# Second FFN of a two-layer decoder: six groups of four hidden blocks by seven products, with the weight sums made ahead and kept in HBM

## The chip, the cores and the metric

The kernel runs on one core of a Trainium2 chip. Its time is the device time of one execution in microseconds; several runs give a median. A profile of one execution says what each engine did: TensorE (PE; its weight loads are PEld), VectorE (DVE), ScalarE (ACT), GpSimd (POOL) and SyncE (SP), which issues most of the transfers.

## The reference

A trunk of two layers over 256 tokens of width 2048, all in float32. Layer 0 mixes tokens by latent attention, layer 1 by dilated sliding-window attention with three head groups; each is followed by a feed-forward network with a short convolution. The part that matters here is that network:

```python
def conv_ffn(h, w_up, conv_w, conv_b, w_down):      # FFN_HIDDEN = 5632, CONV_WIDTH = 3
    u = h @ w_up                                     # 2048 -> 2 x 5632
    up = jnp.pad(u, ((0, 0), (CONV_WIDTH - 1, 0), (0, 0)))
    c = conv_b + up[:, 0:S] * conv_w[0]
    for j in range(1, CONV_WIDTH):
        c = c + up[:, j:j + S] * conv_w[j]
    gate, val = c[..., :FFN_HIDDEN], c[..., FFN_HIDDEN:]
    return (jax.nn.silu(gate) * val) @ w_down

# each layer: x += mixer(rmsnorm(x)); x += conv_ffn(rmsnorm(x)); final rmsnorm
```

## The kernel before

**Precision by splitting.** A float32 weight is used as two halves: `wh`, its value rounded to the fast matmul type (ScalarE copies it, L91), and `wl`, what is left (VectorE subtracts, L92). A product takes three matmuls: high by high, high by low, low by high. The activations are split in the same way and stay in SBUF.

**The weight ring.** `load` (L71 on) takes a tile `w` of 128x2048 (1 MB) from the pool `wst`, which has three, fills it by a transfer on SP's queue (L78), and splits it in two pieces of 1024 columns into `wh` and `wl`, of which the pool `wsp` has five each. A slot of `wst` is free again when VectorE has made the last `wl` from it. `load_tok2` (L146) does so for the value projections of the dilated stage, which come as quarters.

**A direct unit.** `proj` (L137) multiplies one loaded tile, 128 outputs by all 16 chunks of the input, for all 256 tokens: 16 matmuls of 512 columns with `wh` and 16 of 256 columns with `wl`, into one bank `pp` of PSUM. `unit` runs it, takes one entry of the list `steps` (other work to be put between, such as attention), and then empties the bank of the unit before (L213, L215 and what follows).

**The dilated stage** (layer 1's attention) goes over eight pairs of heads j. Each has 12 q and k units (three groups, q and k, two heads). Where j is even, four quarters of a value projection for two pairs follow each group's four units (L165 to L167). The attention of pair j runs from `steps` during pair j+1. Then comes the output projection.

**The FFN** has 44 hidden blocks of 128, each a gate and a value. `up(fb)` does a block by two direct units, the convolution and the gating; `down` adds a segment of some 11 finished blocks to the residual, 16 units, one for each block of outputs. Three groups of four blocks, the *fours* (`SEVEN = (12, 23, 34)`), go another way: the product of a 2x2 block matrix (two halves of the tokens by two halves of the input) with the four blocks' gate and value columns is made by seven block products instead of eight. The sums of activation blocks (`forms`) are made once at the start of the FFN. The sums of weight blocks are made by VectorE as the weights pass (`first`, `second`, L881 to L895), six products running side by side in six PSUM banks, one chunk pair after a `down` unit; the seventh follows (`third`). The products are 512-column matmuls with tokens in the rows (L853 to L855). `sums` and `last_sum` combine them, and `turn` (L947) transposes the result back, four 128x128 blocks for each hidden block, into the bank `pt` or `po`, from which the convolution reads (L958, L962).

**Order.** The framework's scheduler puts each engine's instructions in order before the run and adds the waits; TensorE's order follows the program. Transfers are issued by SP in program order, each waiting for its slot.

Of the kernel before, what the change touches and what calls it, by code (L numbers as in the profile page):

```python
# [40 lines left out]
SEGS = ((0, 10), (10, 21), (21, 32), (32, 44))  # L41
HALF = 4 * P
SEVEN = (12, 23, 34)
NEG = -1.0e30


# [6 lines left out]
def trunk_kernel(tc, x_d, pos_d, gain_d, conv_d, const_d, mask_d, wqa_d, wkva_d, wqb_d, wkvb_d, wo_d,  # L53
                 win_d, dwo_d, wup_d, wdn_d, out_d):
    nc = tc.nc
    with ExitStack() as ctx:
# [5 lines left out]
        tab = ctx.enter_context(tc.tile_pool(name="tab", bufs=1))  # L62
        work = ctx.enter_context(tc.tile_pool(name="work", bufs=4))
        small = ctx.enter_context(tc.tile_pool(name="small", bufs=4))
        pp = ctx.enter_context(tc.tile_pool(name="pp", bufs=4, space=PSUM))
        pss = ctx.enter_context(tc.tile_pool(name="pss", bufs=2, space=PSUM))
        pst = ctx.enter_context(tc.tile_pool(name="pst", bufs=1, space=PSUM))
# [55 lines left out]
        def proj(w, xs, n, since=0, upto=None, ps=None, onto=False):  # L123

            if ps is None:
                ps = pp.tile([P, 512], F32, name="pp", tag="pp")
            ks = range(since, upto or n)
            order = runs()  # L130
            if since == 0:
                state["own", id(ps)] = None if onto else order[0]
            own = state["own", id(ps)]
            for i in order:
                for k in ks:
                    w_k = w[k * P // WS][i][:, k * P % WS:k * P % WS + P]
                    nc.tensor.matmul(ps[:, i * T:], w_k, xs[k][:, :(2 - i) * T], start=(k == 0 and i == own),  # L137
                                     stop=(k == n - 1), skip_group_check=(i != own))
            return ps
# [48 lines left out]

        pending = []
        steps = []  # L190

        def nothing():
            pass
# [9 lines left out]
        def unit(project, evacuate):  # L203
            ps = project()
            if steps:
                steps.pop(0)()
            flush()
            pending.append((evacuate, ps))
# [146 lines left out]
        def split_act(ps):  # L355
            o = act.tile([P, 2 * T], F32R, name="a", tag="a")
            split_to(o, ps)
            return o
# [306 lines left out]
        def dilated():  # L665
# [20 lines left out]
            def project(j):  # L686
                h = {}

                def keep_qk(what, ps):
                    if what[1] == 0:  # L690
                        t = work.tile([P, T], F32, name="qk0", tag="tmp")
                    else:
                        t = att.tile([P, T], F32, name="qk", tag="qk", bufs=8)
                    rope(t, joined(ps), tabs["c"], tabs["s"], 32)
                    if what[1] == 0:
                        h[what] = att.tile([P, 2 * T], F32R, name="qks", tag="qks", bufs=4)
                        split_to(h[what], t)
                    else:
                        h[what] = t

                if j % 2 == 0:
                    state["v"] = {}
                values = h["v"] = state["v"]

                def keep_v(g, pss_):
                    for tt, ps in enumerate(pss_):
                        col = tabs["r"][:, tt:tt + 1]
                        if g == 0:
                            v = att.tile([P, 4 * T], F32R, name="vs", tag="vs", bufs=2)
                            split((v[:, :2 * T], v[:, 2 * T:]), ps, col)  # L710
                        else:
                            v = att.tile([P, 2 * T], F32, name="v", tag="v", bufs=4)
                            nc.scalar.activation(v, ps, AF.Copy, scale=col)
                        values[g, tt] = v

                for g in range(NG):
                    base = (j * NG + g) * 6
                    for i, what in enumerate("qk"):
                        for e in range(2):
                            w = load(win_d[base + 2 * i + e], D, tok=D)  # L720
                            unit(lambda: proj(w, xs, KC), lambda ps, what=what, g=g, e=e: keep_qk((what, g, e), ps))
                    if j % 2 == 0:
                        srcs = [(win_d[b + 4], win_d[b + 5]) for b in (base, base + 6 * NG)]
                        pss_ = [pp.tile([P, 512], F32, name="pp", tag="pp") for _ in range(2)]
                        for q in range(4):
                            w = load_tok2(srcs, q)

                            def quarter():
                                proj_tok2(w, pss_, xs, q)
                                return pss_  # L730

                            unit(quarter, (lambda p, g=g: keep_v(g, p)) if q == 3 else (lambda p: None))
                return h
# [56 lines left out]
                steps.extend([s0, nothing, together(s1, ta0, tb0), nothing, together(v0, ta1, tb1), v1])  # L790
            out_proj(dwo_d, os, G_FFN + KC, onto=True)


        def ffn(layer, goff, ready):
            gl = {}
# [228 lines left out]
            flush()  # L1024


        with tc.tile_pool(name="lat0", bufs=1) as lat, tc.tile_pool(name="att0", bufs=2) as att:
            mla()
        with tc.tile_pool(name="ffn0", bufs=1) as fpool:
# [11 lines left out]
            nc.scalar.activation(xt[c], xt[c], AF.Copy, scale=gains[:, G_FIN + c:G_FIN + c + 1])  # L1041

        with tc.tile_pool(name="ffn1", bufs=1) as fpool:
            ffn(1, G_FFN + KC, final)

        zero = work.tile([P, T], F32, name="zero", tag="lo", bufs=2)
        nc.vector.memset(zero, 0.0)
# [93 lines left out]
```

## Time and profile before

| | |
|---|---|
| three runs | 2674.61, 2674.69, 2675.85 us |
| profiled execution, span from first to last instruction | 2673.9 us |
| TensorE busy | 2657.8 us |
| VectorE busy | 2105.5 us |
| ScalarE busy | 1639.7 us |
| GpSimd busy | 24.7 us |
| mean transfer rate | 189 GB/s |
| read from HBM, written to it | 501.5 MB, 2.1 MB |

A busy share is the part of the span in which at least one instruction of that engine was running. Matmuls are pipelined, so the sum of their durations is longer than their busy time, and the step from one matmul's start to the next tells more than a duration. A row of a window gives its length, then the busy time and count of each engine, the granted clock, the share of the DMA engines' time and the rate. A row of the chain gives start, length and what ran. A row of a wait gives who waited for whom, the sum, the number of times and the longest.

### The profile page before, as it was taken

What the parts mean: (1) busy time and instruction counts of PE and PEld (TensorE: products, weight loads), DVE (VectorE), ACT (ScalarE), POOL (GpSimd) and SP (SyncE); (2) the same over time, 40 slices, a digit from 0 to 9 for tenths busy, and PEclk for the clock granted to TensorE, in tenths of its full rate; (3) what the DMA queues carried; (4) which work ended last, traced back from release to release, by engine and by line L of the source; (5) the groups of instructions that cost most, each with busy time, mean ns of one, the idle gap of its engine ahead of it and who ended that gap; (6) DMA issues with size and microseconds to landing.
All of it is one profiled execution on the core that took longest, in us unless ns stands there. A gap on an engine that the chain in (4) does not pass through costs nothing.

```text
span 2673.9 us, 40017 instructions
## 1 busy us (share of the span) xinstructions
PE 2657.8 (99%) x15167; PEld 2338.4 (87%) x15167; DVE 2105.5 (79%) x3630; ACT 1639.7 (61%) x2624; POOL 24.7 (1%) x39
## 2 busy tenths in 40 slices
PE   9999999999999999999999999999999999999998
PEld 7998888888888888898888888888888888888887
DVE  7987888898898876676577667667688889889885
ACT  6775666676666764444454444445666667666665
POOL 2000000000000000000000000000000000000000
PEclk9999999999999999999999999999999999999999
DMA  6335555656566565544544544544555575755744
GB/s 246 138 133 203 189 182 193 239 179 224 197 202 227 182 206 198 179 171 170 191 170 164 197 161 174 188 174 160 189 189 175 191 249 171 223 205 189 237 169 147
DMA packets 153553, 506.19 MB, mean 189 GB/s; under 512 B 11024, under 2 KB 86160, under 8 KB 118928
## 3 DMA queue, kind: packets, MB, share of 16 engines
q1 hardware_dynamic: 153072, 503.46, 54.9%
q8 instruction: 119, 1.95, 0.3%
q14 instruction: 74, 0.61, 0.1%
q10 hardware_dynamic: 288, 0.18, 0.0%
HBM read 501.50 MB, written 2.10 MB: 188 GB/s over the span
## 4 chain that ended last, share of the span: by engine, by line
PE 95%; DMA 1%; DVE 1%; issue 0%; ACT 0%; SPq 0%; DVEq 0%; ACTq 0%
PE pp L137 70%; PE pp L165 3%; PE pp L167 3%; PE pp L166 3%; PE ps L855 1%; PE ps L853 1%; PE ps L854 1%; DMA w<-in_wup 1%; PE pp L104 1%; PE pp L106 1%; PE pp L105 1%; PE pp L853 1%; PE pp L854 1%; PE pp L855 1%; PE po L781 1%; PE ps L744 1%
## 5 line engine op out<-in xcount | busy, mean ns | idle before, releaser
L92 DVE TENSOR_TENSOR wl<-w,wh 128x1024 fp32r<-128x1024 f32 (+3 forms) x802 | 881.9, 1110 | 371.0 <-ACT wh L91 228.1
L91 ACT ACTIVATE wh<-w 128x1024 fp32r<-128x1024 f32 (+3 forms) x802 | 770.9, 966 | 370.8 <-PE pp L137 220.7
L137 PE MATMUL pp<-xs,wh 128*128 128x512 f32 x3648 | 855.5, 390 | 0.0
L137 PEld LDWEIGHTS pp<-xs,wh 128*128 128x128 f32 x3648 | 677.1, 188 | 135.8 <-DVE xs L266 0.2
L137 PE MATMUL pp<-xs,wl 128*128 128x256 f32 x3648 | 465.3, 284 | 0.0
L137 PEld LDWEIGHTS pp<-xs,wl 128*128 128x128 f32 x3648 | 455.7, 191 | 9.3
L137 PE MATMUL pp<-a,wh 128*128 128x512 f32 x1920 | 459.7, 390 | 0.0
L137 PEld LDWEIGHTS pp<-a,wh 128*128 128x128 f32 x1920 | 357.7, 188 | 72.6
L137 PEld LDWEIGHTS pp<-a,wl 128*128 128x128 f32 x1920 | 248.1, 191 | 10.2
L137 PE MATMUL pp<-a,wl 128*128 128x256 f32 x1920 | 252.8, 283 | 0.0
L155 DVE TENSOR_TENSOR wl<-w,wh 128x1024 fp32r<-128x1024 f32 x96 | 116.2, 1218 | 62.3 <-ACT wh L154 50.3
L154 ACT ACTIVATE wh<-w 128x1024 fp32r<-128x1024 f32 x96 | 101.6, 1059 | 96.5 <-PE pp L166 50.0
L213 ACT ACTIVATE lo<-pp 128x256 f32<-128x256 f32 x225 | 85.7, 381 | 119.5 <-PE pp L137 119.4
L165 PE MATMUL pp<-wh,xs 128*128 128x512 f32 x384 | 150.0, 391 | 0.0
L167 PE MATMUL pp<-wl,xs 128*128 128x512 f32 x384 | 149.5, 389 | 0.0
L166 PE MATMUL pp<-wh,xs 128*128 128x512 f32 x384 | 149.4, 389 | 0.0
L962 DVE SCALAR_TENSOR_TENSOR cv<-upad,convs,cv 128x256 f32<-128x256 f32 x256 | 121.1, 481 | 18.3 <-ACT cv L958 15.9
L958 ACT ACTIVATE cv<-upad,convs 128x256 f32<-128x256 f32 x128 | 76.4, 598 | 72.7 <-DVE upad L972 71.0
L215 DVE TENSOR_TENSOR sum<-pp,lo 128x256 f32<-128x256 f32 x225 | 94.1, 418 | 0.2
L120 ACT ACTIVATE pp<-x 128x512 f32<-128x512 f32 x144 | 85.1, 591 | 13.6 <-DVE sum L215 6.8
L880 ACT ACTIVATE wh<-w 128x1024 fp32r<-128x1024 f32 x48 | 51.0, 1062 | 60.0 <-PE pp L137 43.0
L167 PEld LDWEIGHTS pp<-wl,xs 128*128 128x128 f32 x384 | 72.1, 188 | 15.0
(299 smaller groups left out, 3154.7 us busy)
## 6 DMA issues: line engine op xcount, KB each, us to landing
w<-in_wup SPq DMA_DIRECT2D x128, 1024.0 KB, 4.8
w<-in_win SPq DMA_DIRECT2D x96, 1024.0 KB, 4.8
w<-in_wup SPq DMA_DIRECT2D x96, 512.0 KB, 5.1
w<-in_win SPq DMA_DIRECT2D x96, 512.0 KB, 4.1
w<-in_wdn SPq DMA_DIRECT2D x64, 704.0 KB, 4.1
w<-in_wdn SPq DMA_DIRECT2D x32, 768.0 KB, 4.2
w<-in_wdn SPq DMA_DIRECT2D x32, 640.0 KB, 5.3
w<-in_wo SPq DMA_DIRECT2D x16, 1024.0 KB, 4.7
```

What stands on the lines that cost most here:

```text
L91: nc.scalar.activation(h, w[:, c:e], AF.Copy)
L92: nc.vector.tensor_sub(l, w[:, c:e], h.bitcast(F32))
L120: nc.scalar.activation(dst, chunk.unsqueeze(1).to_broadcast([P, 2, 2, P]), AF.Copy, scale=0.5)
L137: nc.tensor.matmul(ps[:, i * T:], w_k, xs[k][:, :(2 - i) * T], start=(k == 0 and i == own), stop=(k == n - 1), skip_group_check=(i != own))
L154: nc.scalar.activation(wh4, src, AF.Copy)
L155: nc.vector.tensor_sub(wl4, src, wh4.bitcast(F32))
L165: nc.tensor.matmul(ps, xh, wh, start=k == 0, stop=False)
L166: nc.tensor.matmul(ps, xl, wh, start=False, stop=False)
L167: nc.tensor.matmul(ps, xh, wl, start=False, stop=k == KC - 1)
L213: nc.scalar.activation(t, ps[:, T:], AF.Copy)
L215: nc.vector.tensor_add(u, ps[:, :T], t)
L962: nc.vector.scalar_tensor_tensor(o, v, convs[:, cw + j:cw + j + 1], o, op0=ALU.mult, op1=ALU.add)
```

## The change

Layer 0's FFN stays. Layer 1's becomes `ffn_ahead`: six fours go by seven products, two in each of three periods, and 20 blocks directly (12 at the start, 8 as `singles`).

The four sums of weight blocks no longer arise in the FFN. While layer 1's q and k weights are loaded, after every second load, `sums_ahead` takes one more tile of the ring, loads for one hidden block four chunks (512 columns) of each of its four weight parts (gate and value, first and second half of the input) into it by two transfers, adds in place four times on VectorE, and stores the tile to HBM by a transfer from POOL's queue: 48 times, 8 for each four. In the FFN each product then has its weights ready in HBM, raw for products 1, 2 and 3 and summed for 4 to 7. It is done in two halves of 12 matmuls, each with one 1 MB load and one split, the products one after the other in the two `ps` banks. The halves stand after units of `up` and `down`, up to two behind one unit, by lists written out by hand (`deal`, `put`). The 2x2 blocks divide the input in chunks 0 to 7 and 8 to 15 instead of even and odd ones, and the sums have other signs. The transposes stand behind two successive `down` units (7 and 8) for the first four of a period, behind `up` units for the second. At the end three early units of the last `down` replace two.

```diff
+FIRST = 12
+PERIODS = ((0, 11, 12, 16, (20, 21, 22)), (11, 22, 23, 27, (31, 32, 33)), (22, 33, 34, 38, (42, 43)))
...
+        def plan_sums(layer, fours):
+            for fb0 in fours:
+                t = made[layer, fb0] = hbm.tile([8, P, D], F32, name=f"sums_{layer}_{fb0}")
+                ahead.extend((t, layer, fb0, n) for n in range(8))
+
+        def sums_ahead():
+            if not ahead:
+                return
+            t, layer, fb0, n = ahead.pop(0)
+            f, q = n // 2, n % 2
+            w = wst.tile([P, D], F32, name="w", tag="w")
+            for h in range(2):
+                src = wup_d[layer, 2 * (fb0 + f) + h].rearrange("p (j c) -> p j c", j=2)[:, :, q * HALF:(q + 1) * HALF]
+                nc.sync.dma_start(w[:, h * WS:(h + 1) * WS].rearrange("p (j c) -> p j c", j=2), src)
+            b11, b21, b12, b22 = (w[:, ts(i, HALF)] for i in range(4))
+            nc.vector.tensor_add(b11, b11, b12)
+            nc.vector.tensor_add(b12, b12, b22)
+            nc.vector.tensor_add(b22, b11, b22)
+            nc.vector.tensor_add(b21, b22, b21)
+            nc.gpsimd.dma_start(t[n], w)
...
                             w = load(win_d[base + 2 * i + e], D, tok=D)
+                            if e == 0:
+                                sums_ahead()
                             unit(lambda: proj(w, xs, KC), lambda ps, what=what, g=g, e=e: keep_qk((what, g, e), ps))
...
+        def ffn_ahead(layer, goff, ready):
...
+            products = {1: ("a11", (0, 0)), 2: ("a12", (0, 1)), 3: ("s4", (1, 1)), 4: ("a22", 1), 5: ("s1", 0),
+                        6: ("s2", 3), 7: ("s3", 2)}
...
+                def product(i, q):
+                    name, what = products[i]
+                    if q == 0:
+                        ps[i] = pss.tile([P, 512], F32, name="ps", tag="ps")
+                    w = wst.tile([P, D], F32, name="w", tag="w")
...
+                    nc.sync.dma_start(w.rearrange("p (f c) -> p f c", f=4), src.rearrange("f p c -> p f c"))
+                    w5 = w.rearrange("p (f k c) -> p k f c", f=4, k=4)
+                    for h in range(2):
...
+                        nc.scalar.activation(as4(wh), w5[:, 2 * h:2 * h + 2], AF.Copy)
+                        nc.vector.tensor_sub(as4(wl), w5[:, 2 * h:2 * h + 2], as4(wh).bitcast(F32))
+                        for k in range(2):
...
+                            nc.tensor.matmul(ps[i], xh, bh, start=(kk == 0), stop=False)
+                            nc.tensor.matmul(ps[i], xl, bh, start=False, stop=False)
+                            nc.tensor.matmul(ps[i], xh, bl, start=False, stop=(kk == KC // 2 - 1))
...
+                for i in (1, 2, 6, 7, 4, 5, 3):
+                    for q in range(2):
+                        out.append(lambda i=i, q=q: (product(i, q), None if q == 1 else settle()))
...
+            for s, (a, b, one, two, singles) in enumerate(PERIODS):
+                m, settle, turns = seven(one)
+                if s == 0:
+                    deal(m, first[12:], [1] * 12)
+                    deal(m, downs[0], (1, 1))
+                else:
+                    put(ups[s - 1], 0, m.pop(0))
+                    put(ups[s - 1], 1, m.pop(0))
+                    deal(m, ups[s - 1][4:], (1, 1))
+                    deal(m, downs[s], (2, 2, 2, 2, 2))
+                m, settle2, turns2 = seven(two)
+                put(downs[s], 5, settle, m.pop(0))
+                put(downs[s], 6, m.pop(0))
+                put(downs[s], 7, *turns[:2])
+                put(downs[s], 8, *turns[2:])
+                deal(m, downs[s][9:], (2, 2, 1, 2, 2, 1, 2))
+                ups[s][0].insert(0, settle2)
+                ups[s][2] += turns2[:2]
+                put(ups[s], 3, *turns2[2:3])
+                if len(ups[s]) > 4:
+                    put(ups[s], 4, *turns2[3:])
+                else:
+                    put(ups[s], 3, *turns2[3:])
...
+        plan_sums(1, [fb for _, _, one, two, _ in PERIODS for fb in (one, two)])
...
-            ffn(1, G_FFN + KC, final)
+            ffn_ahead(1, G_FFN + KC, final)
```

More of the change, by code (lines that the diff above doesn't have):

```diff
@@ L64, in trunk_kernel @@
         small = ctx.enter_context(tc.tile_pool(name="small", bufs=4))
+        hbm = ctx.enter_context(tc.tile_pool(name="hbm", bufs=1, space=bass.MemoryType.DRAM))
         pp = ctx.enter_context(tc.tile_pool(name="pp", bufs=4, space=PSUM))
@@ L190, in trunk_kernel @@
         steps = []
+        ahead = []
+        made = {}
+        def plan_sums(layer, fours):
[17 more added lines that the diff above has]
+            nc.gpsimd.dma_start(t[n], w)
         def nothing():
```

171 lines of the change are left out of this document (added).

## The prediction

> **What bounds the kernel now.** I read the page first, then the windows by stage, then the chain of waits.
>
> ```profile
> span 2673.9 us, 40017 instructions
> PE 2657.8 (99%) x15167; PEld 2338.4 (87%) x15167; DVE 2105.5 (79%) x3630; ACT 1639.7 (61%) x2624; POOL 24.7 (1%) x39
> ...
> PEclk9999999999999999999999999999999999999999
> ...
> PE 95%; DMA 1%; DVE 1%; issue 0%; ACT 0%; SPq 0%; DVEq 0%; ACTq 0%
> ```
>
> The span is 2673.9 us and the three runs have a median of 2674.69, 0.8 more; differences found in the trace are applied to the median. TensorE is busy nearly throughout at full granted clock, and the chain that ended last is 95% TensorE. Matmuls overlap, though, so their price is read from the chain, where each piece begins as the one before frees the array:
>
> ```profile
> 1032.60 22.23 PE pp L137 x128
> ...
> 2301.10 3.81 PE pp L137 x22
> ...
> 2173.69 0.23 PE ps L853
> ...
> 2176.19 0.23 PE ps L855
> ...
> 2206.92 0.44 PE pt L947 x4
> 2207.36 0.44 PE po L947 x4
> ...
> 2218.90 0.44 PE pt L947 x4
> ```
>
> Four direct units of 32 matmuls take 22.23 us, 5.56 each. A down unit of 11 chunks takes 3.81. Twelve 512-wide matmuls of a product run from 2173.69 to 2176.19 plus one step of 0.23, so 0.2275 each and 2.73 for a half product. Four transposes take 0.44. None of these has a gap in it: TensorE's matmul time is the time, and whatever shortens it shortens the kernel until another engine or a transfer is late.
>
> Now the stages that the change touches. The columns are window, length, PE, PEld, DVE, ACT, POOL busy, clock, share of the DMA engines and GB/s.
>
> ```profile
> 990.50:992.80 2.30, 2.30 (x18) 2.05 (x17) 1.01 (x3) 1.74 (x2) 0.00 (x0) 1.00 1.00 385
> ...
> 1099.00:1196.00 97.00, 97.00 (x555) 85.54 (x554) 68.83 (x134) 47.97 (x67) 0.00 (x0) 1.00 0.50 174
> ...
> 1341.00:1411.00 70.00, 70.00 (x430) 62.88 (x429) 54.63 (x117) 33.50 (x52) 0.00 (x0) 1.00 0.47 166
> ...
> 1945.00:2662.00 717.00, 716.28 (x3984) 626.41 (x3982) 608.94 (x939) 487.93 (x770) 1.33 (x1) 1.00 0.58 195
> ...
> 2162.00:2247.00 85.00, 85.00 (x490) 75.11 (x489) 78.20 (x132) 59.06 (x96) 0.00 (x0) 1.00 0.63 214
> ```
>
> The first is a stretch with all DMA engines busy: 385 GB/s is what they give. The next two lie in the dilated stage where q and k units follow each other without value quarters between them (a "run": all of an odd j and the first four units of the next): VectorE at 71% and 78%, the transfers at half. The fourth is the second FFN, the last a part of it where VectorE is busy 92% of the time and TensorE still never waits.
>
> **The change: what it takes from TensorE.** A four done directly is 8 units, 8 x 5.56 = 44.5 us. By seven products it is 14 halves and 16 transposes, 14 x 2.73 + 4 x 0.44 = 40.0 us. Three more fours go this way: 3 x 4.5 = 13.5 us less. The fours that were already done so keep their count of matmuls. With nothing late the time is 2674.7 - 13.5 = 2661.2. What is left is whether anything becomes late.
>
> **What it adds in the dilated stage.** 48 steps, one at every second q or k load: two 512 KB loads into a tile of the three-slot ring, four adds of 128x512, one 1 MB store from POOL's queue.
>
> ```profile
> L893 DVE TENSOR_TENSOR t<-t,w x48: 681/691/694, 396.5 to 2505.9; 128x512 f32<-128x512 f32 x48
> ...
> L92 DVE TENSOR_TENSOR wl<-w,wh x28: 1197/1225/1227, 1110.6 to 1194.8; 128x1024 fp32r<-128x1024 f32 x28
> ...
> L91 ACT ACTIVATE wh<-w x29: 1049/1060/1062, 1109.5 to 1195.8; 128x1024 fp32r<-128x1024 f32 x29
> ...
> L215 DVE TENSOR_TENSOR sum<-pp,lo 128x256 f32<-128x256 f32 x225 | 94.1, 418 | 0.2
> ...
> w<-in_win SPq DMA_DIRECT2D x96, 1024.0 KB, 4.8
> ...
> w<-in_win SPq DMA_DIRECT2D x96, 512.0 KB, 4.1
> ...
> w<-in_wkva SPq DMA_DIRECT2D x5, 1024.0 KB, 6.4
> ...
> out_y<-x SPq DMA_DIRECT2D x7, 256.0 KB, 2.4
> ...
> L78 SPq DMA_DIRECT2D w<-in_win x16: 327/328/328, 1099.4 to 1190.3; - x16
> ...
> ACT wh L91 <- PE pp L137: 22.7, 17, 3.4
> ...
> SPq L78 <- DVE wl L92: 40.5, 7, 7.8
> ...
> DVE t L881 <- DMA w<-in_wup: 24.1, 25, 2.4
> ...
> POOL rcol L309 <- DVE ms L307: 1623.0, 5, 720.4
> ```
>
> The adds: 4 x 0.69 = 2.75 us, 132 us in all. A run of 16 loads (97 us) gets 8 of them, 22 us: VectorE goes from 68.8 to 91 of 97 us. In the 70 us around an odd j it gets some 6, 16 us, and goes from 54.6 to 71: full. The bytes: 16 MB of loads plus 8 sums of 2 MB are 33.6 MB in 97 us, 346 GB/s, 90% of 385. So nothing passes its limit over a run, but two resources reach it.
>
> What covers this? The waits "ACT wh <- PE" and "SPq <- DVE wl", taken in the first run: ACT waits for TensorE to free one of five split buffers and SP for a slot of the ring. Both buffers are full, and TensorE has up to 2.5 units split ahead, one of which it is working on: some 1.5 units, 8 us, can be lost in a run before TensorE notices, and the value quarters that follow (four units without sums) fill it again. The adds are also VectorE's first touch of a fresh load; such waits today (t <- w) cost 24.1 us in 25, 1 us each. Queued behind such a wait are the splits and the emptying of the last unit's bank; at 1 us each, 8 in a run, it is the cover once over. I take 2 us lost in the whole stage, and bounds of 0 and of the second rival below. SP issues 96 more transfers of 0.33 us, 32 us; in the run it waits 40.5 of 97 us for one releaser alone, a slot freed by VectorE's splits. POOL does nothing between the norms (it waited 1623 us for VectorE), so the stores hold up nobody there.
>
> **What it changes in the second FFN.** VectorE: the old four splits and sums 8 x (4 x 1.22 + 2 x 0.69) + 4 x 1.22 = 55 us, the new one only splits, 28 x 1.22 = 34, a direct one 16 x 1.22 plus two 0.42 us steps a unit, 26. With 7 sums of 0.69, 5 us, per added four: 609 - 3 x 55 + 6 x 34 - 3 x 26 + 3 x 5 = 585 of 703 us, 83% as against 85%. The transfers: 14 MB per four instead of 8 (36 MB more, 38e6 bytes) make (195 x 717 + 37700)/703 = 253 GB/s, 66% of 385. On the mean neither limits. Two places are tight:
>
> - The ring where a down unit is followed by two halves. That takes TensorE 3.81 + 2 x 2.73 = 9.3 us and three tiles; with three slots each may stay 9.3 us. It needs about 4.8 to land and 1.06 + 2 x 1.22 = 3.5 to be split, 8.3. One microsecond is left. Over the 7 units and 12 halves that end a down stage the transfers are 17.6e6 bytes in 59 us, 297 GB/s, 77%. I take no loss; if each tile queued 1.5 us longer, 0.5 us a row, 25 such rows lose 12 less their cover, say 8.
> - The transposes. Two banks (pt and po) take turns for the four blocks of a four. Today the second pair begins 12 us after the first. In the new down stages one down unit lies there, 3.81 us. Rows of VectorE that read the banks today:
>
> ```profile
> 2211.40 0.47 DVE L962 SCALAR_TENSOR_TENSOR cv<-pt,convs,cv 128x255 f32<-128x255 f32 x1
> ...
> 2214.88 0.47 DVE L962 SCALAR_TENSOR_TENSOR cv<-po,convs,cv 128x255 f32<-128x255 f32 x1
> ```
>
> pt is released at 2211.87, 4.5 us after its transposes, po at 2215.35, 7.5 after. With 3.81 us between, the third block would wait 0.3 us and the fourth 2.7: 3 us for each of the three fours in a down stage, 9 us at most, and 0 if VectorE takes the convolutions first. No product half stands in those rows and fewer splits compete, so I take a little over 1 us each, 3.5. In the up stages 5.56 us lie between: nothing.
>
> **Sum.** 2674.7 - 13.5 + 2 + 3.5 = 2666.7, rounded down for the 0.7 us that TensorE idles in the FFN today: 2666.
>
> **Rivals.**
>
> The full gain. Every wait is covered: 2661. For it: the 92% stretch without a stall. Against: TensorE's cover in a run is about what the waits use up.
>
> The sum tile's loop sets the pace of the runs; this one ends slower. Each turn takes three tiles of a three-slot ring, so in rotation a sum tile always gets the same slot, and its load cannot be issued before the last sum's store has landed; the weight load behind it waits on SP too. Turn: 4.1 + 0.33 to land, 2.75 of adds, 1 of waiting, then the store: 2.4 (the 256 KB row) to 6.4 (the slowest 1 MB row), nearest to the 4.8 of the 1 MB loads. That is 10.6 to 14.6, at 4.8 13.0, against 97/8 = 12.1 available. At 13.0 a run falls 7 us behind and the cover takes it. At 14.6 it falls 20 behind and 12 reach TensorE, three times, and 7 in the last run of 12 units: 43 us, 2666 + 41 = 2707. It outweighs the gain from a turn of about 13.4, where three runs lose 2.4 each and the last none, and with the transposes' 9 the gain is gone. Against it: a free slot may be given to whichever tile asks, and then the three stays, 8.3 + 8.3 + 13, come to 10 us a turn. The Trainium skill speaks for the slow end: DMA: Bandwidth & Descriptors, section Bandwidth, gives 6.15 us for a 1 MB load issued from GpSimd, and SBUF — State Buffer, section SBUF: two separate sides, says that descriptors for such a transfer cannot be written while VectorE runs a two-port operation. No run here shows a transfer from POOL; by the page's figure the turn is estimated at 14.3.
>
> The FFN gives it back: transposes 9 and ring 8, less the gain of 13.5: 2678, or with half of it 2671. No measurable change. For it: the 4.5 and 7.5 us above. Against: VectorE has less to do there on the mean than today.
>
> **Chances.** Changes under 0.2%, 5.3 us, can hardly be told from none: faster is below 2669.3, slower above 2680.0. The forecast with small losses (2663 to 2669) 0.40, the full gain 0.17: faster 0.57. The FFN giving it back, or small losses in both places, 0.23. The sum tile's turn 0.20. The faster cases alone reach from 2660 to 2669. For eight in ten the range runs from 2659 to 2690, part of the way to 2707.
>
> **What would show it.** Right: in the dilated stage the chain stays TensorE's, the runs last 97 us within one or two, VectorE is above 90% in them; TensorE's matmuls in the second FFN fall by 3 x (8 x 32 - 14 x 12 - 16) = 216, and the stage shortens from 717 to about 708. Wrong by the sum tile: SP waits on DMA (the store) and TensorE on the splits (wl, wh) in the runs, and these stretch. Wrong by the FFN: TensorE idle before the transposes, or before half products with the releaser "wl" and behind it DMA w. Were VectorE late with the softmax, the transposes of the dilated stage would wait instead.

## The result, and the profile after

| | before | after |
|---|---|---|
| median of the runs | 2674.98 us (4 runs) | 2765.64 us (4 runs, 2760.07 to 2769.82) |
| ratio | | 1.0337, 95% interval 1.0323 to 1.0352 |
| span of the profiled execution | 2673.9 us | 2767.9 us |
| up to the norm before the dilated stage | 993.2 us | 995.7 us |
| dilated stage with its output projection, norm to norm | 950.7 us | 1017.1 us |
| second FFN, norm to norm | 717.0 us | 742.2 us |

Slower by 3.4%, where 0.3% faster was forecast. The 94 us of span are 66.4 us in the dilated stage, 25.2 in the second FFN and 2.5 before both. (Stages are measured between the small matmuls of the norms.)

The page of after; first the span and the busy engines, then the shares of the chain that ended last, then transfers with their number, size and time to land:

```profile
span 2767.9 us, 40168 instructions
PE 2683.1 (97%) x14950; PEld 2329.4 (84%) x14951; DVE 2190.7 (79%) x3760; ACT 1645.3 (59%) x2651; POOL 49.6 (2%) x87
...
PE 54%; DMA 22%; DVE 14%; ACT 3%; issue 3%; SPq 1%; DVEq 0%; ACTq 0%
...
w<-in_win SPq DMA_DIRECT2D x96, 1024.0 KB, 6.8
...
sums<-w POOLq DMA_DIRECT2D x48, 1024.0 KB, 5.0
w<-in_win SPq DMA_DIRECT2D x96, 512.0 KB, 5.8
w<-sums SPq DMA_DIRECT2D x48, 1024.0 KB, 6.4
```

TensorE's matmuls fell from 15167 to 14950, 217 fewer. The chain, 95% TensorE before, is TensorE's for 54% only; transfers have 22% of it and VectorE 14%. A 1 MB weight load of the dilated stage lands after 6.8 us instead of 4.8, a 512 KB one after 5.8 instead of 4.1.

Windows of after, columns as in the prediction: the first run, the dilated stage, the second FFN.

```profile
1099.00:1200.00 101.00, 97.17 (x540) 84.85 (x539) 80.49 (x152) 46.00 (x66) 3.20 (x6) 0.98 0.79 289
990.00:1910.00 920.00, 874.31 (x4741) 757.66 (x4740) 689.21 (x1264) 387.58 (x545) 25.81 (x48) 0.99 0.76 274
2012.80:2755.00 742.20, 718.54 (x3770) 605.99 (x3769) 589.20 (x878) 514.38 (x797) 1.64 (x1) 1.00 0.69 231
```

No engine but TensorE and no queue is full on the mean: VectorE 80% in the run, the DMA engines 79%. TensorE waits all the same, so the loss lies in who waits for whom. The waits in the dilated stage (sum in us, times, longest):

```profile
ACT wh L94 <- DMA w<-in_win: 299.1, 77, 9.2
DVE w L214 <- DMA w<-in_wup: 119.8, 43, 7.1
...
ACT wh L157 <- DMA w<-in_win: 71.0, 31, 5.9
...
PE pp L140 <- DVE wl L95: 25.8, 24, 2.3
```

ScalarE waits 370 us for weights to land, VectorE 120 for the raw parts of the sums (2.8 us each time), and TensorE for VectorE's splits. SP's own queue there names a new releaser, the stores; the three lines are the sum loads, the q and k loads and the value loads:

```profile
SPq L212 <- DMA sums<-w: 52.0, 13, 5.8
...
SPq L81 <- DMA sums<-w: 45.1, 19, 8.6
...
SPq L149 <- DMA sums<-w: 21.3, 9, 3.6
```

One turn of a sum tile can be read off the timelines of POOL, which issues the stores, and of SP, which issues the loads (start, length on the queue):

```profile
1122.32 0.53 POOL L218 DMA_DIRECT2D sums<-w  x1 [30.05 <-DVE w L217]
1135.85 0.53 POOL L218 DMA_DIRECT2D sums<-w  x1 [13.00 <-DVE w L217]
```

```profile
1127.39 1.20 SPq L212 DMA_DIRECT2D w<-in_wup  x2
...
1141.00 1.20 SPq L212 DMA_DIRECT2D w<-in_wup  x2
```

The store issued at 1122.32 landed at 1127.38 and the next sum's load was issued at 1127.39; its parts landed at 1132.56, the adds ran to 1135.5, the store of 1135.85 landed at 1140.99, and at 1141.00 came the next load. That is a turn of 13.6 us. Over the whole stage the median way from a sum's load to the landing of its store was 16.1 us.

In the second FFN, TensorE's timeline shows the two places that the prediction had called tight (the bracket is the idle time before the row and its releaser):

```profile
2348.61 0.50 PE L908 MATMUL ps<-wl,forms 128*128 128x512 f32 x1 [0.52 <-DVE wl L901]
...
2408.95 0.63 PE L952 MATMUL pt<-cst,t 128*128 128x128 f32 x4 [3.35 <-ACT wh L900]
```

### The profile page after: what moved, and what is told of

Read it like the earlier page. It is cut to its first block, busy times and chain, and to the rows that moved or that the text cites. A ratio compares the mean times of both kernels' runs of the same rounds, so it can differ in the third digit from the quotient of the medians.

```text
span 2767.9 us, 40168 instructions
## 1 busy us (share of the span) xinstructions
PE 2683.1 (97%) x14950; PEld 2329.4 (84%) x14951; DVE 2190.7 (79%) x3760; ACT 1645.3 (59%) x2651; POOL 49.6 (2%) x87
## 4 chain that ended last, share of the span: by engine, by line
PE 54%; DMA 22%; DVE 14%; ACT 3%; issue 3%; SPq 1%; DVEq 0%; ACTq 0%
PE pp L140 41%; DMA w<-in_wup 8%; DMA w<-in_win 7%; DMA w<-sums 4%; DMA sums<-w 4%; DVE wl L95 3%; DVE wl L158 2%; DVE wl L901 2%; PE ps L908 1%; PE ps L907 1%; PE ps L906 1%; ACT wh L900 1%; PE pp L107 1%; PE pp L109 1%; PE pp L108 1%
## 5 line engine op out<-in xcount | busy, mean ns | idle before, releaser
L95 DVE TENSOR_TENSOR wl<-w,wh 128x1024 fp32r<-128x1024 f32 x754 | 820.7, 1101 | 234.4 <-ACT wh L94 158.0
L94 ACT ACTIVATE wh<-w 128x1024 fp32r<-128x1024 f32 x754 | 712.5, 959 | 476.6 <-DMA w<-in_win 301.7
L140 PE MATMUL pp<-xs,wh 128*128 128x512 f32 x3264 | 771.6, 392 | 1.2 <-DVE xs L294 1.2
L140 PEld LDWEIGHTS pp<-xs,wh 128*128 128x128 f32 x3264 | 609.4, 189 | 124.2 <-DVE xs L294 1.4
L140 PE MATMUL pp<-a,wh 128*128 128x512 f32 x1920 | 466.0, 392 | 1.3 <-ACT wh L94 1.1
L140 PE MATMUL pp<-xs,wl 128*128 128x256 f32 x3264 | 425.8, 285 | 26.0 <-DVE wl L95 25.8
L140 PEld LDWEIGHTS pp<-xs,wl 128*128 128x128 f32 x3264 | 411.9, 192 | 41.6 <-DVE wl L95 31.4
L140 PEld LDWEIGHTS pp<-a,wl 128*128 128x128 f32 x1920 | 249.8, 192 | 14.1 <-ACT a L380 3.6
L901 DVE TENSOR_TENSOR wl<-w,wh 128x1024 fp32r<-128x1024 f32 x168 | 202.2, 1221 | 73.1 <-ACT wh L900 68.6
L900 ACT ACTIVATE wh<-w 128x1024 fp32r<-128x1024 f32 x168 | 173.4, 1054 | 121.2 <-DMA w<-sums 66.3
L157 ACT ACTIVATE wh<-w 128x1024 fp32r<-128x1024 f32 x96 | 98.4, 1054 | 85.1 <-DMA w<-in_win 71.0
L158 DVE TENSOR_TENSOR wl<-w,wh 128x1024 fp32r<-128x1024 f32 x96 | 114.7, 1209 | 25.3 <-ACT wh L157 25.2
L214 DVE TENSOR_TENSOR w<-w 128x512 f32<-128x512 f32 x48 | 33.2, 691 | 121.1 <-DMA w<-in_wup 121.1
L241 ACT ACTIVATE lo<-pp 128x256 f32<-128x256 f32 x201 | 75.1, 374 | 49.6 <-PE pp L140 49.2
L908 PE MATMUL ps<-wl,forms 128*128 128x512 f32 x192 | 78.1, 407 | 6.9 <-DVE wl L901 6.7
```

Source lines behind the costliest of these rows:

```text
L94: nc.scalar.activation(h, w[:, c:e], AF.Copy)
L95: nc.vector.tensor_sub(l, w[:, c:e], h.bitcast(F32))
L157: nc.scalar.activation(wh4, src, AF.Copy)
L158: nc.vector.tensor_sub(wl4, src, wh4.bitcast(F32))
L900: nc.scalar.activation(as4(wh), w5[:, 2 * h:2 * h + 2], AF.Copy)
L901: nc.vector.tensor_sub(as4(wl), w5[:, 2 * h:2 * h + 2], as4(wh).bitcast(F32))
```

## The experiments

Stages are given as loss against before (950.7 us) for the dilated stage, and for the second FFN as waiting beyond 703.5 us, which is 717.0 less the 13.5 us of matmuls saved. By this measure the change lost 66.4 and 38.7. "Way" is the median time from the issue of a sum's first load to the landing of its store. The first eight versions ran once each, the others four to ten times. Stage losses and waits are those of the profiled execution, which for `after_w44` was its slowest, 2723.1 us. Code is shortened in the diffs.

**The two halves of the change alone.** `dil_only` has the sums of the change and the FFN of before; `ffn_only` has the new FFN without the sums, products 4 to 7 reading raw weights of the same shape where the sums belong (so it computes something else).

```diff
-            ffn_ahead(1, G_FFN + KC, final)
+            ffn(1, G_FFN + KC, final)                      # dil_only
-                t = made[layer, fb0] = hbm.tile([8, P, D], ...); ahead.extend(...)
+                made[layer, fb0] = wup_d[layer, 2 * fb0:2 * fb0 + 8]   # ffn_only
```

> The dilated stage as changed (48 sum steps with store), the second FFN as before; the stored sums are read by nobody. If the two stages lose independently: the loss of the dilated stage alone, 2675 + 69 = 2744, the second FFN at 717. If the FFN's new loads or the dilated stage's lateness carry over into each other: below 2735.

> The second FFN as changed, no sum steps; products 4 to 7 read raw weights of the same shape and place in the access pattern, so the output is not the reference's. Ring theory (three slots, each tile's stay longer than the row allows): the FFN stays at 742, total 2675 - 13.5 + 38.7 = 2700. If reading the freshly stored sums is what is slow (landing 6.4 us against 4.9): the FFN falls towards 704, total 2661 to 2675.

`dil_only` took 2744.26 us: 67.3 lost in the dilated stage, FFN 716.1. `ffn_only` took 2689.57: dilated stage as before, FFN 730.3, so 26.8 us of waiting are the FFN's own and the other 12 come only with the stored sums.

**What in the sums costs: adds or stores.** From `dil_only`, once without the four adds (raw parts are stored), once without the store.

```diff
-            nc.vector.tensor_add(b11, b11, b12)    # and the three others: dil_noadd
-            nc.gpsimd.dma_start(t[n], w)           # dil_nostore
```

> As dil_only, without the four adds: what is loaded is stored as it is (the stored numbers are no sums). Ring theory: the sum tile's turn falls from 13.6 us to about 10.8, under the 12.1 of a pair of units, so most of the loss goes: 2680 to 2695. VectorE theory (the adds fill it): all goes, 2675. Bytes theory (the DMA engines are full): nothing goes, 2744.

> As dil_only, without the store. Ring theory: the turn falls from 13.6 to some 8.3 us, loss nearly gone: 2675 to 2685. VectorE theory: the adds are all there, so the loss stays, about 2744. Bytes theory: half of the added bytes gone, about half of the loss, 2700 to 2715.

Measured 2689.99 us without adds (11.0 lost in the stage), 2674.16 without stores (nothing lost). Windows of `dil_noadd`, then of `dil_nostore` (the run, and the stage):

```profile
1099.00:1196.00 97.00, 97.00 (x556) 85.50 (x555) 66.30 (x130) 44.89 (x64) 3.19 (x6) 1.00 0.81 297
990.00:1842.00 852.00, 843.71 (x4659) 737.08 (x4657) 570.55 (x1050) 385.68 (x534) 25.74 (x48) 1.00 0.79 290
```

```profile
1099.00:1196.00 97.00, 97.00 (x555) 85.53 (x554) 83.78 (x161) 46.80 (x65) 0.00 (x0) 1.00 0.68 242
990.00:1842.00 852.00, 851.73 (x4738) 745.78 (x4737) 695.52 (x1265) 405.32 (x546) 0.69 (x1) 1.00 0.67 237
```

The first has every byte of the change, at a higher rate than the change reached (290 against 274 GB/s), and the run without a stall; so the bytes on the mean are not the limit, though 11 us of the stage remain lost. The second has every add, VectorE at 82% of the stage, and no loss; so VectorE's work is not the limit. SP's waits for stores in `dil_noadd`:

```profile
SPq L81 <- DMA sums<-w: 163.6, 24, 8.9
...
SPq L149 <- DMA sums<-w: 56.5, 12, 7.7
...
SPq L212 <- DMA sums<-w: 52.4, 12, 7.6
```

272 us, over twice the 118 of the change, and it costs little: SP waiting for a store is not enough either. Nor are late weights: without adds ScalarE still waits 207 us for the q and k loads (the line below), at a loss of 11 us.

```profile
ACT wh L94 <- DMA w<-in_win: 206.7, 64, 5.6
```

What only the two together have is VectorE, in the order of its queue, waiting for a raw load that was issued late because a store had not landed. Its waits in `dil_only`, then in `dil_nostore`; without adds there are none:

```profile
DVE w L214 <- DMA w<-in_wup: 123.8, 45, 7.1
```

```profile
DVE w L214 <- DMA w<-in_wup: 32.8, 27, 2.9
```

That both are needed is shown. That these waits are the reason is the reading that fits: without the adds VectorE also has less work, and so more room for late weights.

**A slot for the sums alone, first try.** The sums go to four tiles of the activation pool, loaded by POOL's queue or by SP's, 256 KB at a time, paced by the loads of the whole stage.

```diff
-            w = wst.tile([P, D], F32, name="w", tag="w")
+            b11, b21, b12, b22 = b = [act.tile([P, 2 * T], F32, name="a", tag="a") for _ in range(4)]
...
+                    nc.gpsimd.dma_start(b[2 * h + j], src[:, c:c + HALF])    # dil_own_pool; nc.sync in dil_own_sync
```

> As dil_only, but the sums have tiles of their own (four tiles of the pool act, free until the last pairs of heads), are loaded and stored from POOL's queue, and come at 48 of the first 108 loads. Same bytes, same adds. Ring theory (the sum tile holds a slot of the ring, and SP's queue, until its store has landed): the loss goes, 2675 to 2681. Bytes theory (what was left without the adds, 16 us, is the DMA engines' load): 2690 or more.

> As dil_own_pool, but the sums' loads are issued by SP between the weights' loads, the stores by POOL. If the slot alone was the matter: as dil_own_pool, 2675 to 2681. If SP's queue standing still behind a sum's load was a part of it: 2685 to 2710, with SP waiting on DMA (the store) again.

2772.64 and 2736.1 us. Not the test that it was to be: with no weight ring to hold them, the sums bunched. Two windows of `dil_own_pool`, then one of `dil_own_sync`:

```profile
987.00:1099.00 112.00, 92.58 (x452) 78.87 (x452) 84.07 (x147) 43.23 (x62) 40.33 (x73) 0.91 0.93 328
1099.00:1196.00 97.00, 97.00 (x533) 84.67 (x533) 64.78 (x115) 48.56 (x64) 0.00 (x0) 1.00 0.54 186
```

```profile
987.00:1099.00 112.00, 102.61 (x516) 88.15 (x515) 84.31 (x139) 48.98 (x62) 18.64 (x34) 0.95 0.95 337
```

In these windows the DMA engines are 93 to 95% busy and TensorE loses 9 to 19 of 112 us; where no sums run, nothing. A peak of transfers alone does not explain it, though. Sums also run in the next two windows, `dil_own_pool` and then `dil_own_sync`, with DMA shares of 0.90 and 1.03, and TensorE never stands:

```profile
1200.00:1300.00 100.00, 100.00 (x573) 88.14 (x572) 83.81 (x163) 46.82 (x67) 35.84 (x67) 1.00 0.90 326
```

```profile
1196.00:1220.00 24.00, 24.00 (x147) 21.46 (x145) 21.56 (x42) 9.34 (x12) 5.42 (x10) 1.00 1.03 414
```

One thing that differs between the two long windows of `dil_own_pool` is VectorE's wait for the raw parts, first from 987 to 1099, then from 1200 to 1300:

```profile
DVE a L215 <- DMA a<-in_wup: 28.7, 5, 7.7
```

```profile
DVE a L215 <- DMA a<-in_wup: 6.1, 3, 2.9
```

The window at 414 GB/s holds ten issues of stores beside loads, so the 385 GB/s that the prediction took for all that the DMA engines give, read from 2.3 us, is not a limit.

**The FFN: ring and transposes.** Both from `ffn_only`. `ffn_w44` gives the weight ring four slots, for one split buffer less of each kind; `ffn_turns` sets the transposes further apart.

```diff
-        wst = ... bufs=3        -        wsp = ... bufs=5
+        wst = ... bufs=4        +        wsp = ... bufs=4                  # ffn_w44
-                put(downs[s], 7, *turns[:2])
+                put(downs[s], 6, *turns[:2])                               # ffn_turns
...
+                    put(ups[s], 1, *turns2[:2]); put(ups[s], 2, *turns2[2:])    # last period only
```

> As ffn_only (2690), with four slots in the weight ring and four instead of five split buffers, in the whole kernel; the same SBUF. Ring theory of the FFN (three tiles in a row of 9.3 us, each staying 10 us or more): the waits on wl and wh before half products go, some 10 of the 28 us: 2678 to 2682. If the DMA rate limits there: unchanged, 2690. If five split buffers are what covers VectorE: slower elsewhere too, over 2690.

> As ffn_only (2690), with the transposes placed otherwise: of the four in a down stage two after unit 6 and two after unit 8 (not 7 and 8), of the last four one and two units earlier. If the second pair waits because one down unit is too short for the convolutions that read its banks: the 8 us before pt and the 8 before the last down go, 2674 to 2680. If VectorE or ScalarE is simply behind: the waits move and the time stays within 4 us of 2690.

2677.11 us (FFN 716.2, waiting 12.7 instead of 26.8) and 2679.19 us (717.5, 14.0). TensorE's main wait before the transposes, in the change (sum in us, times, longest):

```profile
PE pt L952 <- ACT wh L900: 6.8, 2, 3.4
```

In `ffn_only` it is 6.9 us, in two waits as well. With four slots it is gone. With the transposes moved it is gone too, but 4.2 us stand before the `po` transposes instead, released by a convolution on VectorE. What held up `pt` can be followed in the change, where the first pair of transposes ended by 2401.3:

```profile
2402.91 1.06 ACT L900 ACTIVATE wh<-w 128x1024 fp32r<-128x1024 f32 x1 [1.99 <-DMA w<-in_wup]
...
2404.14 0.56 ACT L966 ACTIVATE cv<-pt,convs 128x256 f32<-128x256 f32 x1
```

```profile
2408.33 0.47 DVE L970 SCALAR_TENSOR_TENSOR cv<-pt,convs,cv 128x255 f32<-128x255 f32 x1
```

ScalarE's copy out of `pt` stood in its queue behind a split whose load had not landed, VectorE's convolutions start from that copy, and the last of them to read `pt` ended at 2408.8; the next transposes began at 2408.95. The split that the profile names as releaser only ended at the same moment; the transposes read nothing of it.

**Four slots, and all of it together.** `dil_w44` and `after_w44` take the four slots to `dil_only` and to the change; `ffn_w44t` and `after_w44t` add the moved transposes.

> The dilated stage of the change with the FFN of before, and the weight ring given four slots instead of three (the split buffers go from five to four each, so that the space stays the same). A slot then comes round every fourth tile: with three tiles per turn of 12.1 us a sum tile may stay some 16 us instead of 12, against the 13.6 us that its turn took. All transfers and all adds stay. If the slot of the ring sets the pace, the dilated stage loses 0 to 10 us instead of 69: 2675 to 2685. If the bytes are the limit, or VectorE, nothing is changed by a fourth slot: 2735 to 2745. If the four split buffers take away cover, some of the loss stays: 2685 to 2700.

> The whole change with four ring slots and four split buffers of each kind. Ring theory for both stages: dilated stage loses 0 to 10 us instead of 67; the second FFN keeps the 15 us of its last rows and what the longer landing of the stored sums costs, 3 to 10: 2675 to 2690. Bytes theory: dilated stage as in the change, 2735 to 2750.

> The FFN of the change alone (no sum steps; products 4 to 7 read raw weights of the same shape, so the output is not the reference's), with four ring slots and the transposes set further apart (after down units 6 and 8; those of the last four after up rows 1 and 2). The fourth slot alone left 14.8 us of waiting, 10 of it in the last rows where the last four's turns fell late; the moved transposes alone left 16.1, mostly of the ring. If these are two separate causes, together they leave 2 to 6 us: 2663 to 2668. If the last rows are late for another reason, 2674 to 2677 as with four slots alone.

> The whole change with four slots and the transposes set apart: the sum of the parts. If both ring and transposes were the causes, 2663 to 2680, with the longer landing of stored sums deciding within it; below 2669 it beats the kernel before. Bytes theory: 2730 or more.

| | median, us | ratio, 95% | dilated stage lost | FFN waiting |
|---|---|---|---|---|
| `dil_w44` | 2711.3 | 1.0135, 1.012 to 1.015 | 35.0 | (FFN of before) |
| `after_w44` | 2714.3 | 1.0143, 1.0126 to 1.016 | 46.1 | 12.8 |
| `ffn_w44t` | 2669.15 | 0.9975, 0.9966 to 0.9985 | 0.0 | 5.2 |
| `after_w44t` | 2709.69 | 1.0126, 1.0109 to 1.0142 | 38.4 | 6.5 |

In the FFN most of the waiting is gone: with four slots and the transposes apart it waits 5.2 us, and 6.5 with the stored sums, so the 12 us that these cost with three slots are hidden too. The dilated stage did neither what the slot theory (0 to 10) nor what the transfer theory (no change) expected: half of the loss went. In `dil_w44` the way grew to 19.3 us; a store took 6.3 us to land instead of 5.0. ScalarE's waits for q and k weights fell from 288 to 66 us; VectorE's for the sums remained:

```profile
DVE w L214 <- DMA w<-in_wup: 107.1, 47, 5.5
...
ACT wh L94 <- DMA w<-in_win: 66.3, 18, 10.7
```

**Store out of the slot, and sums spread out.** `dil_so` adds into a tile of its own, from which the store reads (three slots, four split buffers); `dil_spread` does a sum step at every third load of the whole stage; `after_w44ts` is `after_w44t` with the sums spread.

```diff
-            nc.vector.tensor_add(b11, b11, b12)     # ... and the store from w
+            nc.vector.tensor_add(o11, b11, b12)     # ... and the store from o          dil_so
-                            if e == 0: sums_ahead()
+                            spread_sums()           # every third load, also after load_tok2   dil_spread
```

> Dilated stage of the change with the FFN of before; three ring slots. The adds now write to a tile of their own, which the store reads (split buffers four instead of five, for the space), so that the sum tile gives its ring slot back after its last add and not after its store has landed. Loads, adds and stores are the same in number and bytes as in the change. Slot theory (the store in the sum tile's stay sets the pace): the stay falls from 13.6 us to load and adds, 5 to 7 and 3 to 4, 8 to 11 of the 12.1 available, and the stage loses 0 to 12 us of its 69: 2675 to 2687. Transfer theory (with 48 MB of stores beside the loads everything lands later, whoever holds the slot; four slots still lost 36): 2705 to 2745.

> Dilated stage of the change with the FFN of before; three ring slots, sum tile stored from its slot as in the change. One sum step at every third load of the whole stage (q, k and value quarters), instead of at every second q or k load in the runs and none at the values: 17.8 us a turn instead of 12.1. With four tiles a turn the slots rotate, and a sum tile may stay three tiles, 13.2 us, against 13.6. Slot theory: nearly all gone, the rest some 0.4 to 1.5 us a turn less cover: 2677 to 2700. Transfer theory on the mean of the stage (same bytes in the same stage, some 290 GB/s): 2720 to 2745. If it is the peak in the runs only, as slot theory.

> The whole change with four slots, transposes set apart, and a sum step at every third load of the dilated stage. With four slots and four tiles a turn a sum tile has one slot for itself and may stay 17.5 us; with four slots and the sums in the runs its stay was 17 to 22, the adds lying between splits. Slot theory: dilated stage loses 0 to 12 us instead of 39: 2670 to 2683. Transfer theory: no change from the version with the sums in the runs, 2705 to 2712.

2760.78 us (ratio 1.0315, 1.0298 to 1.0332), 2750.79 (1.0278, 1.0263 to 1.0293) and 2730.97 (1.0211, 1.0196 to 1.0227). In the dilated stage they lost 57.1, 73.0 and 62.0 us (`dil_so` lost another 31 elsewhere, where four split buffers with three slots were too few). All three missed both ranges of the slot theory. Waits of `dil_so`, then of `dil_spread`:

```profile
ACT wh L94 <- DMA w<-in_win: 202.6, 55, 8.0
DVE so L216 <- DMA w<-in_wup: 147.8, 43, 8.4
```

```profile
ACT wh L94 <- DMA w<-in_win: 248.4, 72, 6.8
ACT wh L157 <- DMA w<-in_win: 138.5, 34, 7.1
...
DVE w L214 <- DMA w<-in_wup: 59.0, 34, 6.7
```

In `dil_so` the slot was freed by the last add, 13.3 us after the load instead of 16.4; but now the next sum's load could be under way beside the store and a weight load, a sum's parts landed after 8.6 us and its store after 9.1, and VectorE waited more. In `dil_spread` the way was 19.6 us; VectorE waited less and the weights came later. Neither kind of wait went.

**Five slots.** `dil_w53`, `after_w53ts`: `wst` with five tiles, `wsp` with three.

> Dilated stage of the change with the FFN of before, five ring slots and three split buffers of each kind (same space). With three tiles a turn of 12.1 us a sum tile may stay 5/3 turns, 20.2 us. Its measured way from the issue of its load to the landing of its store was 16.4 us with three slots (12.1 allowed, 69 us lost) and 19.3 with four (16.1 allowed, 36 lost). Chain theory (load, adds in VectorE's order and store, one after the other in one slot, against what the ring allows): 19 to 20 against 20.2, 0 to 20 us lost: 2675 to 2695. Transfer theory (346 GB/s wanted in the runs, more than mixed loads and stores get): as with four slots or worse, 2705 to 2715. If three split buffers are too few, TensorE waits for splits while VectorE is free, and the loss is of another kind.

> The whole change with five ring slots, three split buffers, transposes set apart and a sum step at every third load. Four tiles a turn of 17.6 us: a sum tile may stay 5/4 turns, 22 us, against a way of 19.2 measured with four slots (17.6 allowed, 62 lost). Chain theory: dilated stage loses 0 to 15 us; the second FFN takes 708 to 715: 2665 to 2685. Transfer theory: 2705 to 2730, since bytes and adds are as before.

2744.0 us (1.0262, 1.0245 to 1.0279) and 2753.18 (1.029, 1.0275 to 1.0305): 51.3 and 66.3 lost in the stage. SP's waits for sum loads, VectorE's, and one stall of TensorE in `dil_w53`:

```profile
SPq L212 <- DMA sums<-w: 75.3, 15, 11.1
```

```profile
DVE w L214 <- DMA w<-in_wup: 115.7, 43, 11.9
```

```profile
1426.58 2.07 PE L140 MATMUL pp<-xs,wl 128*128 128x256 f32 x8 [7.19 <-DVE wl L95]
```

This stall shows the chain whole. A store issued at 1406.26 took until 1417.07 beside two weight loads. SP, with the next sum's load in front, waited for it from 1405.97 on, 11.1 us; the load landed at 1424.6. VectorE had the first add next and stood 11.6 us, the splits behind it, and TensorE lost 7.2. But why did that load wait for the sum just before, with five slots? Slots are given out before the run, and not in rotation. In `dil_w53` the load that waits for a store comes 3 to 5 tiles after that sum's own load, as in `dil_w44`; in the change 2 to 4. A fifth slot lengthened nothing, and the expectation, which reckoned with rotation, tested nothing there.

**A slot that no weight shares.** `after_own1f`: the sum tile has a pool of one in the dilated stage (its ring stays at three for weights, four split buffers; elsewhere the ring has the fourth), a step at every 10/3 loads up to the end of the output projection, the next load released by a tiny GpSimd instruction.

```diff
-            w = wst.tile([P, D], F32, name="w", tag="w")
+            w = sumt.tile([P, D], F32, name="w", tag="w")
+            nc.gpsimd.tensor_add(w[:, 0:2], *[made["last"][-1][0][:, 0:2].bitcast(F32)] * 2)
```

> The whole change with the sum tile in a slot of its own in the dilated stage (ring of three for the weights alone, split buffers four), one sum step at every 10/3 loads of the dilated stage and its output projection (19.8 us a turn), the load of the next sum released by GpSimd, which does nothing else there, so that no weight load is put into a slot that waits for a store. In the other stages the fourth tile serves the ring, and the transposes are set apart. Way of a sum tile so far 16 to 19 us. Chain theory (loads wait in SP's queue for a store to land, then VectorE in its order waits for the late loads): neither happens any more, the dilated stage and its projection lose 0 to 15 us instead of 69, the second FFN takes 708 to 715: 2665 to 2685. If it is the transfers themselves (all bytes kept) or VectorE's work: 30 or more lost in the dilated stage, 2695 to 2735.

2717.24 us, ratio 1.0155 (1.014 to 1.017): 37.8 lost in the dilated stage. (The FFN took 720.6 us, some 11 more than in `after_w44t`; the reason was not followed up.) VectorE's and ScalarE's waits, and SP's:

```profile
DVE w L223 <- DMA w<-in_wup: 151.0, 42, 9.0
...
ACT wh L102 <- DMA w<-in_win: 21.8, 12, 4.0
```

```profile
SPq L221 <- DMA sums<-w: 157.8, 43, 7.7
```

Weight loads no longer wait for stores, and ScalarE hardly waits for weights. The sums' loads still stood at the head of SP's queue until a store landed, 3.7 us each time (and 63 us in all for the GpSimd instruction), and VectorE waited 3.6 us for each. So more than half of the loss stays when weights and sums share no slot. The other 28 us can't be put down to the shared slot alone, since the pace and the split buffers changed too.

## Why the prediction was wrong

**TensorE saves 13.5 us: right.** The page counts 217 matmuls fewer, where 216 were forecast, and the FFN of `ffn_w44t` takes 708.7 us against the 703.5 that this gives.

**Covers in the dilated stage, "I take 2 us lost": wrong, 66.4.** This step failed, and most of the miss is here. The bytes and VectorE's load were weighed each against its limit, and each was rightly found below it: `dil_noadd` and `dil_nostore` show both. What was not weighed is that they form one chain through queues kept in order. A late store holds SP, SP's late load holds VectorE, and VectorE's wait holds the splits. The wait for a fresh load was put at 1 us from today's row (24.1 in 25); it measured 2.8, and the weights landed after 6.8 instead of 4.8 us. VectorE's account of a run fits: 84 us of work (`dil_nostore`) and eight waits of 2.75 (124 in 45 of `dil_only`) make 106 of 97 us, and the three stretches of the change that hold a run, from one value quarter to the next, grew by 8 to 12 us. That account is an argument; that adds and stores must come together is shown.

**The rival "the sum tile's loop" had the mechanism, at a chance of 0.20 and with too small a price.** Its signs came as listed: SP waiting for the store, TensorE for the splits, runs stretched. The turn was 13.6 us in the first run, between its 13.0 and 14.6, made of a load of 5.2 (4.4 assumed), adds of 2.8 and a store of 5.1; its break-even was 13.4. But it counted losses in the runs alone, 41 us, and had the rest of the stage recover; the stretches with value quarters lost too: the even j took 146.1 to 150.9 us from the second on, instead of 140.2. And it explained the turn by the slot in rotation. Slots do not rotate, and a version with a slot of its own still lost 38 us. The objection held against it, that a free slot may go to whoever asks, was true and did not help.

For the store, the Trainium skill (DMA: Bandwidth & Descriptors, section Bandwidth) gives 6.15 us for 1 MB issued from GpSimd, for a load; the 48 stores here took 5.0 in the median, 9.1 in `dil_so`. Of the Trainium skill's other rule (SBUF — State Buffer, section SBUF: two separate sides), that descriptors cannot be written while VectorE runs a two-port operation, no run shows a sign, nor whether VectorE ran any here: GpSimd's issue took 0.53 us in the rows above, and the stores landed as fast as loads.

**The second FFN, 0 for the ring and 3.5 for the transposes: wrong, 38.7 us of waiting.** The ring's term took 4.8 us to land. With other loads in flight on three slots it measured 6.6 to 7.1, so a tile stays some 10.3 us with its split of 3.5, longer than the 9.3 of a row. The rows of one down unit and two halves that can be told apart took 10.2 us in the median (15 rows of the change, 9.3 to 11.2). The worst case was 1.5 us more on each tile and 0.5 a row; it came to some 2 and 0.9. The transposes' term took it that `pt` is released 4.5 us after its transposes, as today; in the rows above it was 8. It was worked out from VectorE's convolutions without ScalarE's copy, on which they wait, and this copy stood behind a split that waited for a load. The two terms are not separate: four slots take 14.1 us away and moving the transposes 12.8, both together 21.6, since a late load is behind both. The stored sums landed later than raw halves (6.2 us against 5.1, each alone in flight, in five and two loads), which was not foreseen; the 12 us that come with them on three slots fit that, and why they land later is open.

**What stays open.** About 38 us of the dilated stage remain with a slot of its own, and 35 with four slots. VectorE's waits of 107 to 151 us remain in these versions; no run took them away while keeping both adds and stores (adds on GpSimd were not tried), so whether they account for the whole rest is not settled, nor how much of them comes from crowded transfers. None of the versions that have the sums and use them beat the kernel before: the FFN's part is worth about 6 us (`ffn_w44t`), the sums cost at least 35 as placed here.

## What to carry to other kernels

Add up a chain of load, work and store along the queues that it passes, and not only the load of each resource: an engine at 80% can lose time when it takes, in its own order, something that another queue delivers late. A transfer's time to land must be taken under the traffic that the change makes (6.8 us here, not 4.8), and a wait for a fresh load priced on every instruction queued behind it, on each engine. A ring slot that a store must release is late for whoever the scheduler gave it to, which more slots need not cure (four halved the loss here, five did less). Removing the store and removing the work, one at a time, told in two runs what no mean showed.

## What the runs showed of the hardware

- Loads and stores together reached 414 GB/s for 24 us (`dil_own_sync`, the row above), more than the 385 of the short stretch of loads in the prediction, and TensorE did not stand in it.
- How long a transfer takes to land goes with what else is under way, in medians: a 1 MB q or k load took 4.8 us before, 5.9 in `dil_noadd` and 6.8 in the change; a 1 MB store took 5.0 in the change and 9.1 in `dil_so`.
- The granted clock falls at the stalls of TensorE, and it never fell in these stages of the kernel before. The rows of `dil_w53` around the stall above show it; within the first it was 0.50 from 1424 to 1432:

```profile
1420.00:1440.00 20.00, 12.41 (x54) 10.70 (x55) 13.97 (x27) 4.78 (x6) 0.53 (x1) 0.74 0.70 251
1440.00:1460.00 20.00, 20.00 (x126) 18.09 (x125) 18.21 (x40) 7.89 (x13) 0.53 (x1) 1.00 0.96 349
```

The fall follows the waits, but it costs time of its own. While the clock is at 0.5, matmuls of 512 columns that follow each other step by 0.427 us instead of 0.2275, and those of 256 columns by 0.213 instead of 0.119. In the dilated stage of the change this holds for 27 us, in seven stretches, and the longer steps add up to some 9 of the 66 us lost. So a stall costs more than its own length.
